# An output product in which 6 of 16 row pairs are done as seven block products instead of eight

## The chip, the cores and the metric

The kernel runs on one core of one Trainium2 chip. The metric is the device time of one execution in microseconds (us). TensorE (PE) multiplies, VectorE (DVE) and ScalarE (ACT) work elementwise, SyncE (SP) starts most transfers. Each engine works through its own list of instructions in order. The list is the order in which the program's text records them, so an instruction that waits holds back everything behind it on its engine.

## The reference, cut to what matters

One layer of a bidirectional encoder for 256 positions of width 4096. A normalised input is multiplied by `w_in` (4096 x 14336), the columns go to a convolution branch and an attention branch, and the two results, 2048 columns each and each multiplied by a gate, are multiplied together with `w_out`:

```python
h = einsum('bsd,de->bse', rms_norm(x, norm_g), w_in)
c_val, c_glu, c_gate, q, k, v, a_gate = split(h, split_pts, axis=-1)
conv_out = conformer_conv(c_val, c_glu, ...) * silu(c_gate)
attn_out = longnet_mixture(norm(q), norm(k), v, rel_bias) * silu(a_gate)
mixed = concatenate([conv_out, attn_out], axis=-1)      # 256 x 4096
x = x + einsum('bse,ed->bsd', mixed, w_out)             # the output product
```

Everything is float32.

## The kernel before, in words

**Products.** The contraction of 4096 is cut into 32 steps of 128 (`KT`), the columns into 18 groups of 1024 (`GROUPS`: 4 conv, 4 pairs of agv and qk, 2 gate, 4 out). A step of a group reads a 128x1024 piece of the weights (`raw`, loaded in pairs of steps, 1 MB each, three buffers) and makes 12 matmuls of 128x512: two halves of the columns (`e`), two halves of the positions (`s`), and three products each. The three come from a split of each float32 operand into a rounded high part and a low remainder: high by high, low by high, high by low. The stationary side is the 128x128 slice of the activations (`xh`, `xl` in the input groups, `mh`, `ml` in the out groups), the moving side the weights (`wh`, `wl`).

**The split of the weights.** `split_w` (L189) does it three steps ahead: ACT rounds 128x1024 into `wh` (L197), DVE subtracts to get `wl` (L198). There are four buffers of each, so a cast for a later step waits until PE has used up the buffer of an earlier one.

**Side work.** Between the steps `pump()` (L539) records a portion of the elementwise work: lanes of generators, each with a budget of DVE and ACT time per step (`DVE_STEP`, `ACT_STEP` = 950, 1400 ns). The order of the lanes is `mix_lane` (the split of the mixed columns), `fg` (three generators wide: attention heads and gates), `conv_lane`. Gates, queries and keys are turned into the other layout by `turn` (L289): two DVE transposes and 16 ACT copies.

**The out groups.** The mixed columns become `mh`, `ml` (`mix_split_gen`, L522), 32 tiles of 128x256, in the order 0 to 31, each as soon as the last input group has given its buffer free. The four out groups accumulate in PSUM over all 32 steps, in `acc` banks. At a group's end `add_out` (L552) adds the bank to the input tile `xr` on DVE and sends it out.

Of the kernel before, what the change touches and what calls it, by code (L numbers as in the profile page):

```python
# [32 lines left out]
DVE_STEP, ACT_STEP = 950, 1400  # L33
# [13 lines left out]
GROUPS += [("out", og, 1024 * og, 1024 * og + 512) for og in range(4)]  # L47

# [56 lines left out]
def layer_kernel(  # L105
# [8 lines left out]
    out,  # L114
# [58 lines left out]
    def load_pair(j, cuts=(0, 2048), between=None):  # L173
# [4 lines left out]
        if groups[g][0] == "out":  # L178
            jj = (jj + n_pairs // 2) % n_pairs
# [8 lines left out]

    def split_w(n):  # L189
        if n >= NG * KT:  # L190
            return
        j, kk = divmod(n, 2)
        src = raw_tiles[j][:, kk]
        wh = sb.tile([P, 1024], F32R, tag="wh", bufs=AHEAD + 1, name=f"wh{n}")
        wl = sb.tile([P, 1024], F32R, tag="wl", bufs=AHEAD + 1, name=f"wl{n}")
# [96 lines left out]
    def turn(tile_, name, flip=False):  # L292
# [226 lines left out]

    def mix_split_gen():  # L520
        for kk in range(KT):
            while not (kk in mix_ready and progress["in"] >= kk + 2):  # L522
                yield
            h, l = new_split(kk, "m")
            src = mix_ready[kk]
            nc.scalar.copy(h, src)
            nc.vector.tensor_sub(l, src, h.bitcast(F32))
            mh[kk], ml[kk] = h, l
            yield 335

    fg, mix_lane, conv_lane = Lane(3), Lane(1), Lane(1)
# [19 lines left out]
    def add_out(g, e, s, acc, queues=(nc.sync,)):  # L551

        c, n = groups[g][2 + e], 512 // len(queues)
        for i, queue in enumerate(queues):
            t = xr_tiles[(g, e)][:, s, n * i : n * i + n]
            nc.vector.tensor_add(t, t, acc[:, n * i : n * i + n])  # L556
            queue.dma_start(out[0][P * s : P * s + P, c + n * i : c + n * i + n], t)

    def evacuate(g, e, accs):
        kind, idx = groups[g][:2]  # L560
        rstd = state.get("rstd")
        if kind == "out":
            for s in range(2):
                add_out(g, e, s, accs[s])
            return
# [20 lines left out]
        elif kind == "gate":  # L586
            fg.add(gate_post(2 * idx + e, tile_))
# [14 lines left out]
    def last_products(n):  # L602

        g, k = divmod(n, KT)
        wh, wl = (t[:, 512:] for t in w_split[n])
        for s in range(2):
            a = accs[(g, 1)][s]
            hs, ls = (t[:, P * s : P * s + P] for t in (mh[k], ml[k]))
            nc.tensor.matmul(a, hs, wh, start=False, stop=False)
            nc.tensor.matmul(a, ls, wh, start=False, stop=False)  # L610
            nc.tensor.matmul(a, hs, wl, start=False, stop=True)
            add_out(g, 1, s, a, (nc.scalar, nc.sync) if s else (nc.sync,))

    def products(n, e, part):
# [6 lines left out]
        if g < n_in:  # L621
            h, l = xh[k], xl[k]
        else:
            while k not in mh:
                pump()
            h, l = mh[k], ml[k]
# [9 lines left out]
        if part == 1:  # L636
            if k == KT - 1:
                evacuate(g, e, accs.pop((g, e)))
            if e == 1:
                del w_split[n]  # L640

# [16 lines left out]
    for n in range(NG * KT):  # L658
        g, k = divmod(n, KT)
        if g == n_in - 1:  # L660
            progress["in"] = k
        elif g >= n_in:
            progress["in"] = KT + 2
        if groups[g][0] == "out" and k in (8, 12):
            e = (k - 8) // 4
            c = groups[g][2 + e]
            t = t4(f"xr{g}_{e}").rearrange("p a b -> p (a b)").rearrange("p (s c) -> p s c", s=2)
            nc.sync.dma_start(t, xs[:, :, c : c + 512])
            xr_tiles[(g, e)] = t
# [8 lines left out]
        else:  # L678
# [8 lines left out]
            split_w(n + AHEAD)  # L687
            if k < KT - 1:
                products(n, 0, 1)
            elif n < NG * KT - 1:  # L690
                products(n, 1, 0)
                products(n, 1, 1)
            else:
                last_products(n)
# [13 lines left out]


# [58 lines left out]
```

## Time and profile before

| what | us |
|---|---|
| median of three runs | 1610.34 (1609.34 to 1611.03) |
| the profiled execution, its own time | 1610.65 |
| its span, first to last instruction | 1608.9 |
| PE busy | 1602.5 |
| DVE busy | 1072.5 |
| ACT busy | 926.4 |
| out groups on PE | from 1256.4 to 1604.6 |

The profile was taken in one execution. The time outside the span (1610.65 less 1608.9) is start and end of the program. A busy PE in this profile only says that matmuls follow each other; their pace is read from their starts.

### The profile page before, as it was taken

The numbers are of one execution on the slowest core, as the hardware profiler recorded it, in microseconds if no ns is written. First come the engines' busy times: TensorE is split into PE (matmuls) and PEld (weight loads), VectorE is DVE, ScalarE is ACT, GpSimd is POOL, SyncE is SP. The second block draws the span as 40 slices with busy tenths as digits, with TensorE's granted clock in tenths as the row PEclk, the third lists the DMA queues.
The fourth block names the chain that finished last, engine by engine and source line by source line (L and its number), as shares of the span: only waits on it lengthen the run. The fifth ranks groups of instructions, "written<-read, shape, count | busy, mean of one in ns | idle before, by whom it ended". The sixth has DMA issues, their size and how long they took to land.

```text
span 1608.9 us, 18840 instructions
## 1 busy us (share of the span) xinstructions
PE 1602.5 (100%) x7058; PEld 1326.6 (82%) x7058; DVE 1072.5 (67%) x1442; ACT 926.4 (58%) x1413; POOL 0.2 (0%) x4
## 2 busy tenths in 40 slices
PE   9999999999999999999999999999999999999999
PEld 7888888888888888888888888888888888888887
DVE  6658888888888888678756555555465665454543
ACT  6763544545453456774778756774767963333332
POOL 0000000000000000000000000000000000000000
PEclk9999999999999999999999999999999999999999
DMA  9755555555555555545555555455555556566662
GB/s 372 291 185 201 191 189 203 185 185 206 187 205 184 196 197 193 193 168 199 185 195 187 187 198 197 174 189 202 184 198 188 196 204 231 207 228 216 216 229 105
DMA packets 52892, 323.53 MB, mean 201 GB/s; under 512 B 5792, under 2 KB 8480, under 8 KB 16192
## 3 DMA queue, kind: packets, MB, share of 16 engines
q1 hardware_dynamic: 52512, 322.05, 56.0%
q8 instruction: 55, 0.90, 0.2%
q10 hardware_dynamic: 288, 0.28, 0.1%
q14 instruction: 37, 0.30, 0.1%
HBM read 318.08 MB, written 4.23 MB: 200 GB/s over the span
## 4 chain that ended last, share of the span: by engine, by line
PE 98%; ACT 1%; DMA 0%; issue 0%; DVE 0%; DVEq 0%
PE acc L632 32%; PE acc L633 32%; PE acc L635 32%; PE psc L469 1%; PE po L508 1%; ACT cT L394 0%; ACT wh L197 0%; DMA first_x<-in_x_cols_dram 0%; ACT qk L308 0%; DVE wl L198 0%; DVE xr L556 0%; DVE qk L449 0%; ACT xh L245 0%; PE vapm L366 0%; PE mupm L366 0%
## 5 line engine op out<-in xcount | busy, mean ns | idle before, releaser
L198 DVE TENSOR_TENSOR wl<-raw,wh 128x1024 fp32r<-128x1024 f32 x575 | 703.6, 1224 | 514.3 <-ACT wh L197 510.4
L197 ACT CAST wh<-raw 128x1024 fp32r<-128x1024 f32 x575 | 604.9, 1053 | 638.4 <-PE acc L633 449.4
L632 PE MATMUL acc<-wh,xh 128*128 128x512 f32 x1792 | 703.9, 393 | 1.0 <-ACT xh L245 1.0
L633 PE MATMUL acc<-wh,xl 128*128 128x512 f32 x1792 | 698.6, 390 | 0.0
L635 PE MATMUL acc<-wl,xh 128*128 128x512 f32 x1792 | 484.1, 389 | 0.0
L632 PEld LDWEIGHTS acc<-wh,xh 128*128 128x128 f32 x1792 | 336.9, 188 | 71.0 <-ACT xh L245 1.3
L633 PEld LDWEIGHTS acc<-wh,xl 128*128 128x128 f32 x1792 | 337.0, 188 | 70.4 <-DVE xl L246 0.2
L635 PEld LDWEIGHTS acc<-wl,xh 128*128 128x128 f32 x1792 | 336.8, 188 | 70.5
L340 DVE SCALAR_TENSOR_TENSOR cT<-conv,wT,cT 128x241 f32<-128x241 f32 (+14 forms) x480 | 201.6, 471 | 0.0
L632 PE MATMUL acc<-wh,mh 128*128 128x512 f32 x510 | 198.4, 389 | 0.0
L633 PE MATMUL acc<-wh,ml 128*128 128x512 f32 x510 | 198.4, 389 | 0.0
L635 PE MATMUL acc<-wl,mh 128*128 128x512 f32 x510 | 137.5, 389 | 0.0
L633 PEld LDWEIGHTS acc<-wh,ml 128*128 128x128 f32 x510 | 95.8, 188 | 19.9
L635 PEld LDWEIGHTS acc<-wl,mh 128*128 128x128 f32 x510 | 95.7, 188 | 19.8
L632 PEld LDWEIGHTS acc<-wh,mh 128*128 128x128 f32 x510 | 95.7, 188 | 19.8
L499 ACT COPY pr<-turn_p 32x128 f32<-32x128 f32 x256 | 75.9, 296 | 5.9 <-DVE turn_p L493 2.4
L308 ACT COPY qk<-turn_q 32x256 f32<-32x256 f32 x64 | 25.9, 404 | 1.2
L308 ACT COPY qk<-turn_k 32x256 f32<-32x256 f32 x64 | 25.8, 403 | 1.2 <-DVE turn_k L300 0.2
L308 ACT COPY gate<-turn_g 32x256 f32<-32x256 f32 x64 | 25.9, 404 | 1.0
L308 ACT COPY agv<-turn_ag 32x256 f32<-32x256 f32 x64 | 25.8, 404 | 1.0
L308 ACT COPY conv<-turn_a 32x256 f32<-32x256 f32 x64 | 25.8, 403 | 1.1
L483 ACT ACTIVATE pr<-pr,nm 128x256 f32<-128x256 f32 x32 | 16.0, 502 | 2.5 <-DVE nm L480 2.4
(128 smaller groups left out, 402.2 us busy)
## 6 DMA issues: line engine op xcount, KB each, us to landing
raw<-in_w_dram SPq DMA_DIRECT2D x286, 1024.0 KB, 4.8
x<-in_x_dram SPq DMA_DIRECT2D x8, 512.0 KB, 7.4
xr<-in_x_dram SPq DMA_DIRECT2D x8, 512.0 KB, 5.8
out_dram<-xr SPq DMA_DIRECT2D x15, 256.0 KB, 5.2
xT<-in_x_cols_dram SPq DMA_DIRECT2D x7, 512.0 KB, 7.3
T<-bias_dram SPq DMA_DIRECT2D x16, 192.0 KB, 5.0
raw<-in_w_dram SPq DMA_DIRECT2D x3, 512.0 KB, 6.5
raw<-in_w_dram SPq DMA_DIRECT2D x2, 256.0 KB, 4.2
```

The source lines that it names most:

```text
L197: nc.scalar.copy(wh, src)
L198: nc.vector.tensor_sub(wl, src, wh.bitcast(F32))
L308: nc.scalar.copy(dst[32 * b : 32 * b + 32, :, :, to, :], backwards(v) if flip else v)
L340: nc.vector.scalar_tensor_tensor(c[:, t, lo:hi], a[:, t, lo + sh : hi + sh], wT[:, ch, k : k + 1], c[:, t, lo:hi], op0=ALU.mult, op1=ALU.add,)
L469: nc.tensor.matmul(psc[:, it, :], qt[hg][:, hh, P * it : P * it + P], kt[hg][:, hh, :], start=True, stop=True,)
L483: nc.scalar.activation(pi[:, it, :], pi[:, it, :], AF.Exp, bias=nm[:, it : it + 1], accum_out=z[:, it : it + 1],)
L499: nc.scalar.copy(dst[32 * b : 32 * b + 32, :, :, 3 - a, :], backwards(blocks[32 * a : 32 * a + 32, :, :, b, :]),)
L508: nc.tensor.matmul(po[:, :S], vt[hg][:, jt, hs], pT[:, jt, :], start=jt == 0, stop=jt == 1)
L632: nc.tensor.matmul(a, hs, wp, start=k == 0, stop=False)
L633: nc.tensor.matmul(a, ls, wp, start=False, stop=False)
L635: nc.tensor.matmul(a, hs, wp, start=False, stop=k == KT - 1)
```

## The change

The output product is written anew as a class `Out`. The rows of `w_out` are taken as 16 pairs of steps, and a pair, a column group and both position halves are a 2x2 by 2x2 block product: positions (2 halves) by steps (2), steps (2) by column halves (2). In ten pairs it stays eight block products (24 matmuls). In the six pairs 0 to 5 (heads 0 to 11) it becomes seven (21 matmuls), on sums and differences of the blocks. The weights' sums are made in each group on DVE (`t13`, `t24`), the activations' sums once (`mix_fuse`). Four of the seven results have banks of their own, m1, m5, m6 and m7, and `add_more` adds them to the right outputs after the last of the six pairs. The buffers of `wh` and `wl` become one ring of eight (`ws`), and two more buffers are taken from another pool from the eleventh pair of the first group on. The side work changes too: gates have a lane of their own ahead of `fg`, the split of mixed columns takes whatever pair is ready, in the order of use, up to twice per `pump`, and stands behind `fg`; during the two gate groups the budgets are 1300 and 1600; `turn` reports its copies in units of four instead of two.

The core of the diff:

```diff
-DVE_STEP, ACT_STEP = 950, 1400
+STEP, GATE_STEP = (950, 1400), (1300, 1600)
...
+FUSED = (0, 1, 2, 3, 4, 5)
+OUT_ORDERS = [(8, 9, 10, 0, 6, 1, 11, 2, 7, 3, 12, 4, 13, 5, 14, 15)]
+OUT_ORDERS += 3 * [(8, 9, 0, 10, 1, 11, 2, 6, 3, 7, 4, 12, 5, 13, 14, 15)]
+W_SLOTS, W_MORE = 8, 2
...
-                if a % 2 == 1:
-                    yield 0, 620
+            yield 0, 1240
...
+    def mix_fuse(j):
+        a0, a1 = mix_ready[2 * j], mix_ready[2 * j + 1]
+        a11, a21, a12, a22 = a0[:, :P], a0[:, P:], a1[:, :P], a1[:, P:]
...
+        nc.vector.tensor_add(s1, a21, a22)
+        nc.vector.tensor_sub(s2, s1, a11)
+        yield 400
+        nc.vector.tensor_sub(s3, a11, a21)
+        nc.vector.tensor_sub(s4, a12, s2)
+        yield 400
...
+        for (h, l), src in zip(parts, (a11, s1, a1, sums[:, P:])):
             nc.scalar.copy(h, src)
             nc.vector.tensor_sub(l, src, h.bitcast(F32))
+            yield 300, 300
...
     def pump():
-        for i, quota in enumerate((DVE_STEP, ACT_STEP)):
+        for i, quota in enumerate(GATE_STEP if progress["in"] >= 0 else STEP):
             left[i] = min(left[i] + quota, quota)
-        mix_lane.step(left)
+        gate_lane.step(left)
         fg.step(left)
+        for _ in range(2):
+            mix_lane.step(left)
...
+    class Out:
...
+        def step(self, most=W_SLOTS):
+            if not self.todo or sum(self.held.values()) + self.todo[0][0] > most:
+                return False
...
+        def split_plain(self, u):
+            def part(k):
...
+                nc.scalar.copy(h, src)
+                nc.vector.tensor_sub(l, src, h.bitcast(F32))
...
+        def split_fused(self, u):
...
+            def one():
...
+                nc.vector.tensor_sub(t13, r[:, 1:4:2, :], r[:, 0:2, :])
+                h, l = both("b", r[:, 0:3:2, :])
+                low(h, l, r[:, 0:3:2, :])
...
+            def two():
...
+                h, l = both("t13", t13)
+                nc.vector.tensor_sub(t24[:, 0, :], r[:, 3, :], t13[:, 0, :])
+                low(h, l, t13)
...
+            def three():
+                nc.vector.tensor_sub(t24[:, 1, :], r[:, 2, :], t24[:, 0, :])
...
+                nc.scalar.copy(hl[:, 0, :], r[:, 3, :])
+                low(hl[:, 0, :], hl[:, 1, :], r[:, 3, :])
...
+            def four():
+                h, l = both("t24", kept["t24"])
+                low(h, l, kept["t24"])
...
+        def triple(self, acc, a, b, start, stop):
+            nc.tensor.matmul(acc, a[0], b[0], start=start, stop=False)
+            nc.tensor.matmul(acc, a[1], b[0], start=False, stop=False)
+            nc.tensor.matmul(acc, a[0], b[1], start=False, stop=stop)
+        def before(self):
+            while self.step(W_SLOTS + (W_MORE if self.settled else 0)):
+                pass
...
+            rows = (
+                (more["m1"], "a11", "b11", ""), (one["c11"], "a12", "b21", "b"),
+                (more["m5"], "s1", "t1", ""), (more["m7"], "s3", "t3", "t13"),
+                (one["c12"], "s4", "b22", "b22"),
+                (more["m6"], "s2", "t2", ""), (one["c21"], "a22", "t4", "t24"),
+            )
...
+        def add_more(self, g, more):
...
+            nc.scalar.copy(m1, more["m1"])
+            nc.vector.tensor_add(r[0][1], r[0][1], more["m5"])
+            nc.vector.tensor_add(r[1][1], r[1][1], more["m5"])
+            nc.vector.tensor_add(u, m1, more["m6"])
+            nc.vector.tensor_add(v, u, more["m7"])
+            for dst, src in ((r[0][0], m1), (r[0][1], u), (r[1][0], v), (r[1][1], v)):
+                nc.vector.tensor_add(dst, dst, src)
```

**PE in an out group.** Before, 12 matmuls in a row in the third out group, as many as a step has; a pair has two such lists (`acc` the four banks, `wh` and `wl` the split weights, `mh` and `ml` the split mixed columns):

```order
L632 MATMUL acc_0_0_10991<-wh_11241,mh_9838 128x512
L633 MATMUL acc_0_0_10991<-wh_11241,ml_9839 128x512
L632 MATMUL acc_0_1_10992<-wh_11241,mh_9838 128x512
L633 MATMUL acc_0_1_10992<-wh_11241,ml_9839 128x512
L632 MATMUL acc_1_0_11009<-wh_11225,mh_9812 128x512
L633 MATMUL acc_1_0_11009<-wh_11225,ml_9813 128x512
L632 MATMUL acc_1_1_11010<-wh_11225,mh_9812 128x512
L633 MATMUL acc_1_1_11010<-wh_11225,ml_9813 128x512
L635 MATMUL acc_1_0_11009<-wl_11226,mh_9812 128x512
L635 MATMUL acc_1_1_11010<-wl_11226,mh_9812 128x512
L635 MATMUL acc_0_0_10991<-wl_11242,mh_9838 128x512
L635 MATMUL acc_0_1_10992<-wl_11242,mh_9838 128x512
```

Of the change, in the first out group, the last four of the seven block products of pair 0 (`m` a bank of its own, `c` a bank of the output, `mx` the split sums of the mixed columns):

```order
L782 MATMUL m_0_9979<-t13h_9921,mx_9228 128x512
L783 MATMUL m_0_9979<-t13h_9921,mx_9228 128x512
L784 MATMUL m_0_9979<-t13l_9922,mx_9228 128x512
L782 MATMUL c_0_9817<-b22s_9948,mx_9228 128x512
L783 MATMUL c_0_9817<-b22s_9948,mx_9228 128x512
L784 MATMUL c_0_9817<-b22s_9948,mx_9228 128x512
L782 MATMUL m_0_9978<-t24h_9980,mx_9228 128x512
L783 MATMUL m_0_9978<-t24h_9980,mx_9228 128x512
L784 MATMUL m_0_9978<-t24l_9981,mx_9228 128x512
L782 MATMUL c_0_9816<-t24h_9980,mh_9226 128x512
L783 MATMUL c_0_9816<-t24h_9980,ml_9227 128x512
L784 MATMUL c_0_9816<-t24l_9981,mh_9226 128x512
```

The matmuls keep their shape and come in threes into one bank; such a pair has 21 of them, and the whole list of PE has 72 fewer.

**DVE in the second out group.** Before, the list holds only the low parts, two for each pair:

```order
L198 TENSOR_TENSOR wl_11294<-raw_11211,wh_11293 128x1024
L198 TENSOR_TENSOR wl_11310<-raw_11211,wh_11309 128x1024
L198 TENSOR_TENSOR wl_11328<-raw_11245,wh_11327 128x1024
L198 TENSOR_TENSOR wl_11344<-raw_11245,wh_11343 128x1024
L198 TENSOR_TENSOR wl_11362<-raw_11279,wh_11361 128x1024
```

Of the change, one fused pair and the plain pair behind it (`t_20` are the sums t13 and t24, `b22s` holds the high and the low part of one block, `oh` and `ol` the split of a plain pair):

```order
L748 TENSOR_TENSOR t_20_10667<-raw_10569 128x1024
L736 TENSOR_TENSOR bl_10670<-raw_10569,bh_10669 128x1024
L759 TENSOR_TENSOR t_20_10676<-raw_10569,t_20_10667 128x512
L736 TENSOR_TENSOR t13l_10678<-t_20_10667,t13h_10677 128x1024
L765 TENSOR_TENSOR t_20_10676<-raw_10569,t_20_10676 128x512
L736 TENSOR_TENSOR b22s_10689<-raw_10569,b22s_10689 128x512
L736 TENSOR_TENSOR t24l_10705<-t_20_10676,t24h_10704 128x1024
L717 TENSOR_TENSOR ol_0_10723<-raw_10627,oh_0_10722 128x1024
L717 TENSOR_TENSOR ol_1_10733<-raw_10627,oh_1_10732 128x1024
```

Seven instructions now stand where two stood; the low part of t24 comes last and needs ACT's high part of the sum that DVE made two places ahead.

**ACT at the first fused pair of the first out group.** Of the change (`turn_g` is the turned gate, `mix_sums` and `agv` feed the split of the mixed columns, `t_3` the sums of the weights):

```order
L732 CAST bh_9898<-raw_9770 128x1024
L315 COPY gate_0_9789<-turn_g_9837 32x2x4x32 x4
L570 CAST mx_9867<-mix_sums_9841 128x384
L732 CAST t13h_9921<-t_3_9896 128x1024
L315 COPY gate_0_9789<-turn_g_9837 32x2x4x32 x4
L767 CAST b22s_9948<-raw_9770 128x512
L315 COPY gate_0_9789<-turn_g_9837 32x2x4x32 x4
L570 CAST mh_9967<-agv_0_6233 128x128
L570 CAST mh_9967<-mix_sums_9942 128x128
L732 CAST t24h_9980<-t_3_9920 128x1024
```

The casts that PE needs now share ACT's list with the copies of the third gate and the casts of the mixed columns' sums.

More of the change, by code (lines that the diff above doesn't have):

```diff
@@ L113, in layer_kernel @@
     bias_rows,
-    out,
+    y,
 ):
@@ L657, in layer_kernel @@
     split_w(1)
-    for n in range(NG * KT):
+    for n in range(n_in * KT):
         g, k = divmod(n, KT)
[L660 to L669, printed above, removed]
+        if groups[g][0] == "gate":
+            progress["in"] = max(k - KT * (n_in - 1 - g), 0)
         if n == 0:
@@ L707, in layer_kernel @@
         pump()
+    progress["in"] = KT + 2
+    out.run()
 def _layout(i):
```

222 lines of the change are left out of this document (184 added, 38 removed).

## The prediction

> **What bounds the kernel now.** First the busy times and the chain of work that ended last, from the page:
>
> ```profile
> PE 1602.5 (100%) x7058; PEld 1326.6 (82%) x7058; DVE 1072.5 (67%) x1442; ACT 926.4 (58%) x1413; POOL 0.2 (0%) x4
> PE 98%; ACT 1%; DMA 0%; issue 0%; DVE 0%; DVEq 0%
> ```
>
> A busy PE proves little in this profile, since pipelined matmuls count as busy. So next the waits, asked for PE alone. These are all there are:
>
> ```profile
> PE spin L653 <- DVE ones L136: 1.0, 1, 1.0
> PE acc L632 <- ACT xh L245: 1.0, 1, 1.0
> PE psc L469 <- DVE qk L449: 0.4, 1, 0.4
> ```
>
> In the out groups PE waits for nothing. Its pace there comes from the first and the last start, with the counts (510 + 510 + 510 + 6 = 1536 matmuls):
>
> ```profile
> L632 PE MATMUL acc<-wh,mh x510: 389/389/389, 1256.6 to 1602.5; 128*128 128x512 f32 x170
> L611 PE MATMUL acc<-wl,mh x2: 388/388/389, 1603.9 to 1604.6; 128*128 128x512 f32 x2
> ```
>
> 348.0 us over 1535 intervals is **226.7 ns for each matmul**. The 389 ns is one matmul's latency, not its pace. PE is the bound, and a matmul less is 226.7 ns less, as long as its operands are there.
>
> Whether they stay there is a question for DVE and ACT, stage by stage: the last gate group, then the four out groups (columns: PE, PEld, DVE, ACT, POOL busy us):
>
> ```profile
> 1165.00:1256.40 91.40, 91.40 (x404) 75.64 (x404) 56.52 (x77) 69.63 (x148) 0.00 (x0) 1.00 0.51 182
> 1256.40:1343.50 87.10, 87.10 (x386) 72.12 (x385) 54.84 (x74) 63.01 (x108) 0.00 (x0) 1.00 0.59 207
> 1343.50:1430.60 87.10, 87.10 (x386) 72.13 (x385) 41.58 (x37) 33.82 (x33) 0.00 (x0) 1.00 0.62 218
> 1430.60:1517.70 87.10, 87.10 (x386) 72.13 (x385) 41.58 (x37) 33.81 (x33) 0.00 (x0) 1.00 0.62 217
> 1517.70:1604.80 87.10, 87.10 (x385) 71.90 (x384) 39.16 (x35) 30.39 (x29) 0.00 (x0) 1.00 0.52 185
> ```
>
> DVE is half idle in three out groups and carries leftover side work in the first. This room is what the change spends.
>
> **What is removed.** Six pairs in four groups lose three matmuls each: 6 x 4 x 3 = 72, and 72 x 226.7 ns = **16.3 us**. A group then has 366 matmuls, 83.0 us. The new ones have the old shape. They come in threes into one bank; the nearest rows are the last six of before, which do that:
>
> ```profile
> 1604.11 0.39 PE L609 MATMUL acc<-wh,mh 128*128 128x512 f32 x1
> 1604.34 0.39 PE L610 MATMUL acc<-wh,ml 128*128 128x512 f32 x1
> 1604.57 0.39 PE L611 MATMUL acc<-wl,mh 128*128 128x512 f32 x1
> ```
>
> They start 0.23 us apart, to the two digits shown. I take the same pace, and keep for the upper end 0.0013 us for each of the 1464 matmuls, 1.9 us.
>
> **What is added on DVE.** Prices by width:
>
> ```profile
> L198 DVE TENSOR_TENSOR wl<-raw,wh 128x1024 fp32r<-128x1024 f32 x575 | 703.6, 1224 | 514.3 <-ACT wh L197 510.4 <-PE acc L635 1.9 <-PE acc L633 1.5
> L205 DVE TENSOR_TENSOR wl<-raw,wh 128x512 fp32r<-128x512 f32 x2 | 1.3, 683 | 0.0
> L527 DVE TENSOR_TENSOR ml<-agv,mh 128x256 fp32r<-128x256 f32 x16 | 6.7, 418 | 0.0
> L300 DVE STREAM_TRANSPOSE turn_g<-gate 128x512 f32<-128x512 f32 x8 | 5.6, 699 | 0.0
> L197 ACT CAST wh<-raw 128x1024 fp32r<-128x1024 f32 x575 | 604.9, 1053 | 638.4 <-PE acc L633 449.4 <-DVE cT L340 149.8 <-issue 13.0
> L203 ACT CAST wh<-raw 128x512 fp32r<-128x512 f32 x1 | 0.6, 627 | 0.3 <-DMA raw<-in_w_dram 0.3
> ```
>
> A plain pair costs DVE 2 x 1.224 = 2.45 us. A fused pair costs 4 x 1.224 + 3 x 0.683 = 6.95 us; ACT pays 3 x 1.053 + 0.627 = 3.79. Fused and plain pairs alternate in the middle of a group: 9.39 us of DVE beside 45 matmuls, 10.20 us of PE. On top comes a wait inside the fused pair: ACT's cast of t24 can start only when DVE has made the second half of t24, and DVE has one 0.683 us instruction to do meanwhile: 1.053 - 0.683 and two hand-overs of 0.04 (the cast that starts at 1450.40 below ends at 1451.45, the subtraction starts at 1451.49) make 0.45 us.
>
> ```profile
> 1450.40 1.05 ACT L197 CAST wh<-raw 128x1024 fp32r<-128x1024 f32 x1 [1.67 <-PE acc L633]
> 1451.49 1.23 DVE L198 TENSOR_TENSOR wl<-raw,wh 128x1024 fp32r<-128x1024 f32 x1 [1.50 <-ACT wh L197]
> ```
>
> So 9.84 of 10.20 us are taken: **groups two to four fit, with 0.36 us left per two pairs**. By group it is 41.58 + 6 x 4.50 + 8 x 0.683 (add_more) = 74.0 us against 83.0. A gain or loss elsewhere on ACT costs nothing there: 33.8 + 6 x 1.68 + 0.63 = 44.5 us.
>
> **The first out group does not fit.** Counted in DVE's list between its first matmul and its last: 44 instructions of 1024 columns, 26 of 512, 4 transposes, 19 of 256, 13 of 128 and 3 of 384. The last two widths are not in the trace; by the step from 256 to 512 (0.265 us) they are 0.29 and 0.55. The sum is 53.9 + 17.8 + 2.8 + 7.9 + 3.8 + 1.7 = **87.9 us**; with six waits of 0.45, 90.6, against 83.0 of PE: 7.6 us too much. The excess is no early debt that is paid back within the group; the second group opens with four `add_out` (2.7 us) and fused pairs from its third on, so DVE stays late.
>
> What covers it is how far ahead DVE may work, the ring of eight. With the tiles in order of use (four of a plain pair, seven of a fused), the low part of t24 goes where the high part of the plain pair's second step was, whose last use is matmul 44 of the 45; it is first needed by matmul 63. That is 18 matmuls, 4.1 us, and the next plain pair's first low part has 18 too. With ten tiles the tightest has 24, 5.4 us. DVE may be late by that much before PE stops.
>
> ACT adds to the lateness. Before, in the first 44 us of the out groups, it was already full, and PE did not wait:
>
> ```profile
> 1254.00:1265.00 11.00, 11.00 (x50) 9.09 (x49) 6.81 (x8) 10.73 (x21) 0.00 (x0) 1.00 0.45 157
> 1265.00:1276.00 11.00, 11.00 (x50) 9.11 (x49) 8.24 (x14) 9.86 (x18) 0.00 (x0) 1.00 0.59 220
> 1276.00:1287.00 11.00, 11.00 (x50) 9.10 (x49) 7.08 (x9) 10.66 (x21) 0.00 (x0) 1.00 0.67 244
> 1287.00:1298.00 11.00, 11.00 (x50) 9.12 (x49) 7.34 (x13) 10.71 (x22) 0.00 (x0) 1.00 0.67 239
> ```
>
> Now the copies of the third gate stand between the casts of the first fused pair, and DVE, which could once run past, needs those casts in order. I take between 0 and 2 us of DVE time lost there, and 1.0 as the value.
>
> Stalls of PE in the first group and at the start of the second: 7.6 + 1.0 - 4.1 = **4.5 us**, in many pieces of less than 2 us. Bounds: 0 (the work ahead and the ten tiles cover all) and 10 (nothing covered).
>
> **The last gate group.** By the lists it gets about 10 us more on each engine (DVE 56.5 to 67, ACT 69.6 to 79 of 91.4). These are the casts and sums of pairs 0 to 2 and a gate that is turned earlier. A late cast there has 28 matmuls, 6.3 us, from the last use of its buffer to its own use; the running excess of ACT over PE, added step by step from the list, peaks at 4.4. I take no cost, with 0 to 2 us.
>
> **Edits at nothing.** The loads of weights keep their number, and 1 MB lands in 4.8 us where a buffer of three has more than 9. `add_more` (5.5 us of DVE) stands where three to five plain pairs follow, which leave DVE 3 us each. The mixed columns are recorded at least two pairs ahead of use. If one of these covers were gone, PE would wait for that one instruction, 1 to 2 us. The tail, last matmul to the end, has the same two halves and queues.
>
> ```profile
> raw<-in_w_dram SPq DMA_DIRECT2D x286, 1024.0 KB, 4.8
> ```
>
> **Sum.** 1610.65 (1608.9 of span and 1.75 around it) - 16.3 + 4.5 = **1598.8 us**. The profiled execution is 0.3 above the median of the three runs; that is within the runs' own spread, and I leave it.
>
> **The rivals.**
>
> *All is covered.* DVE starts the out groups with nothing outstanding and the larger budgets have emptied the lanes. Against it: 7.6 us of excess is more than either cover. Time: 1610.65 - 16.3 = 1594.3.
>
> *A jam of ACT and DVE.* Casts late in the gate group and in the first out group add up and nothing is made good: 10 us instead of 4.5: 1604.
>
> *One long stall.* If the lateness falls on one wait, PE restarts slowly. The trace has one such restart, after the wait at the start:
>
> ```profile
> 5.41 0.80 PE L632 MATMUL acc<-wh,xh 128*128 128x512 f32 x1 [1.02 <-ACT xh L245]
> 6.00 0.73 PE L633 MATMUL acc<-wh,xl 128*128 128x512 f32 x1
> 6.53 0.63 PE L632 MATMUL acc<-wh,xh 128*128 128x512 f32 x1
> 6.96 0.63 PE L633 MATMUL acc<-wh,xl 128*128 128x512 f32 x1
> 7.38 0.63 PE L632 MATMUL acc<-wh,xh 128*128 128x512 f32 x1
> 7.81 0.63 PE L633 MATMUL acc<-wh,xl 128*128 128x512 f32 x1
> 8.23 0.63 PE L632 MATMUL acc<-wh,xh 128*128 128x512 f32 x1
> 8.66 0.63 PE L633 MATMUL acc<-wh,xl 128*128 128x512 f32 x1
> 9.09 1.47 PE L635 MATMUL acc<-wl,xh 128*128 128x512 f32 x4
> 10.39 0.39 PE L632 MATMUL acc<-wh,xh 128*128 128x512 f32 x1
> ```
>
> They start 0.43 us apart before they fall to 0.227. The twelve ahead of 10.39 took 4.98 us instead of 2.72: 2.3 us, so 1601.1. The windows show a granted clock of 1.00 in every stage here, so nothing but the start bears on it, and my stalls are short. The Trainium skill, in "TensorE: Matmul & The Clock Gate" (section "Why this matters for your kernels"), says that a gap of PE over about 3 us sends the clock back to half; that speaks against any change that trades matmuls for waits. By that rule single stalls below its limit cost only themselves, which leaves the sum at 1598.8. The slow start at 5.41 agrees with it in size; a gap in mid-kernel is not shown here.
>
> *DVE becomes the bound in all four groups (slower).* The place is the wait for t24's cast. The 0.45 us holds only if ACT is free at that moment and the other casts stay hidden. A fused pair may lose 0.81 us (10.20 - 9.39) before each further bit is paid 24 times. At 1.49 us (0.81 + 16.3/24) the whole gain is gone. If the cast of t13 is exposed too (1.053 + 0.08), the loss is 1.58 us or a little over; at 1.7 it is 24 x 0.89 = 21.4 us more than 1594.3: 1615.7. For it: DVE waited for such casts 501 times before, 510.4 us. Against it: that was an idle engine early at its post, and behind t13's cast DVE has 1.224 us of other work.
>
> That the matmuls are not removed can be excluded: PE's list has 72 rows fewer.
>
> **How the numbers follow.** Forecast 0.58, all covered 0.13, jam 0.10, long stall 0.06, DVE bound everywhere 0.13. The predicted time is the forecast's. The range takes in full cover (1594.3) and the upper bounds together (10 of stalls, 1.9 of pace, less a little): 1594 to 1607, and leaves out the DVE bound and little else. A measurement of this kernel tells about 0.2%, 3.2 us, from no change: faster is below 1607.1. All of the forecast but 0.01, full cover, nearly all of the jam and the long stall, and a little of the last rival make 0.86; the rest is 0.06 for the same and 0.08 for slower, both mostly the last rival.
>
> **What would show it.** The profile after should have PE's pace at 0.227 in the out groups, DVE near 88 us in the first of them and 74 in the second and third, waits of PE for DVE's low parts (t24's, and the plain pair's behind it) of 2 to 8 us in all, from the fourth pair of the first group to about the fourth of the second, and none in the gate groups. Waits spread over all groups would mean the last rival; waits for ACT in the gate group the jam; starts 0.43 us apart the long stall. Wrong altogether would be a pace that is not 0.227, or a fused pair that costs DVE more than 7.4 us.

## The result, and the profile after

The changed kernel takes **1603.47 us** (median, 1603.11 to 1603.91), the kernel before on the same chip 1610.31 (1609.34 to 1611.03). The ratio is **0.9959, 95% interval 0.9944 to 0.9973**: faster by 0.4%, 6.8 us, of the 16.3 us that the removed matmuls are worth. The profiled execution took 1603.12 us, with a span of 1601.3. One disturbed execution, of e5 below (2692.08 us at a granted clock of 0.557, one of five), is left out of its median.

First the busy times and the chain, from the page of the changed kernel:

```profile
PE 1590.5 (99%) x6986; PEld 1312.8 (82%) x6986; DVE 1195.0 (75%) x1630; ACT 968.2 (60%) x1480; POOL 0.2 (0%) x4
PE 96%; ACT 1%; DVE 1%; issue 0%; DMA 0%; DVEq 0%; ACTq 0%
```

PE has 72 matmuls fewer (7058 - 6986). The first and last start in the out groups, from the instructions by line:

```profile
L782 PE MATMUL c<-oh,mh x320: 387/389/628, 1257.8 to 1596.5; 128*128 128x512 f32 x160
L784 PE MATMUL c<-ol,mh x320: 388/389/628, 1258.2 to 1597.0; 128*128 128x512 f32 x160
```

The out groups last from 1257.8 to 1597.0. 1463 intervals of 0.2267 us would be 331.7 of these 339.2 us, so **7.5 us are lost in the out groups**. They also start 1.1 us later than before (1257.8 against 1256.6 us, first matmul against first matmul; the 1256.4 in the table of before is the weight load ahead of it). -16.3 + 7.5 + 1.1 is -7.7 us; the spans differ by -7.6.

Which stages lose it? The last gate group and the four out groups (columns: PE, PEld, DVE, ACT, POOL busy us, granted clock, DMA share, GB/s):

```profile
1165.00:1257.80 92.80, 92.03 (x404) 75.21 (x403) 63.91 (x109) 79.91 (x175) 0.00 (x0) 1.00 0.51 180
1257.80:1348.30 90.50, 86.91 (x367) 69.16 (x366) 80.89 (x110) 62.35 (x99) 0.00 (x0) 0.98 0.53 194
1348.30:1431.30 83.00, 83.00 (x368) 68.70 (x367) 72.19 (x78) 42.78 (x46) 0.00 (x0) 1.00 0.69 245
1431.30:1514.30 83.00, 83.00 (x368) 68.73 (x367) 70.15 (x74) 43.08 (x46) 0.00 (x0) 1.00 0.64 228
1514.30:1597.30 83.00, 83.00 (x367) 68.46 (x365) 66.74 (x71) 39.10 (x42) 0.00 (x0) 1.00 0.50 179
```

The windows are cut at each group's first matmul. Groups two to four take 83.0 us each, and PE never pauses in them. The first takes 90.5: all 7.5 us are there. Its DVE is busy for 80.9 us, less than PE would need without a pause (83.0); ACT is idle for 28 us. Over the whole group no engine is full, and yet PE waits. But DVE is nearly full: its 9.6 idle us are all waits for ACT (10.2 us by the list of waits, the largest of them below), so its work and these waits fill the group between them. PE's waits behind 1150 us:

```profile
PE m L782 <- ACT t24h L732: 1.2, 1, 1.2
PE m L784 <- DVE t24l L736: 1.1, 3, 0.5
PE po L514 <- ACT pr L505: 0.8, 2, 0.5
PE c L782 <- ACT oh L716: 0.5, 1, 0.5
PE c L784 <- DVE ol L717: 0.5, 1, 0.5
PE m L784 <- DVE t13l L736: 0.2, 1, 0.2
```

The waits for `pr` (turned attention weights) are in the gate group, the others in the first out group. The listed waits of the first out group, 3.5 us, are shorter than the loss. A wait is counted from the modelled end of the matmul before, which is later than the next start at full pace; the start behind it follows after 0.33 to 0.34 us instead of 0.227; and behind two of the waits several starts stand 0.43 us apart (last section). What held DVE and ACT back there, over 1257 to 1345 us:

```profile
DVE t24l L736 <- ACT t24h L732: 4.1, 5, 2.0
DVE ol L717 <- ACT oh L716: 3.5, 4, 1.3
```

```profile
ACT mh L547 <- DVE cT L416: 10.3, 5, 3.4
ACT t24h L732 <- DVE t L765: 4.9, 3, 2.0
```

**DVE waits for ACT, and ACT waits for DVE.** ACT's list around the largest of these waits shows how:

```profile
1284.29 0.41 ACT L547 CAST mh<-cT 128x256 fp32r<-128x256 f32 x1 [3.43 <-DVE cT L416]
1284.60 1.05 ACT L732 CAST t13h<-t 128x1024 fp32r<-128x1024 f32 x1
1285.55 0.61 ACT L767 CAST b22s<-raw 128x512 fp32r<-128x512 f32 x1
1287.27 0.41 ACT L547 CAST mh<-cT 128x256 fp32r<-128x256 f32 x1 [1.11 <-DVE cT L416]
1288.81 0.41 ACT L547 CAST mh<-cT 128x256 fp32r<-128x256 f32 x1 [1.13 <-DVE cT L416]
1289.12 1.04 ACT L732 CAST t24h<-t 128x1024 fp32r<-128x1024 f32 x1
```

The cast of a mixed column stands in ACT's list behind the DVE multiplication by the gate that makes it (L416), which DVE has recorded behind the weights' subtractions. ACT waits 3.43, 1.11 and 1.13 us for it, and the casts that PE needs next (`t13h`, `t24h`) stand behind it. PE stops for `t24h` until 1290.22 and for `t24l` until 1291.48 (its rows are in the last section).

A second place has another cause. The copies of a turn stand between the casts of one fused pair, and DVE meets them at `t24h`:

```profile
1307.35 1.65 ACT L315 COPY gate<-turn_g 32x256 f32<-32x256 f32 x4
1309.03 0.62 ACT L767 CAST b22s<-raw 128x512 fp32r<-128x512 f32 x1
1309.67 1.65 ACT L315 COPY gate<-turn_g 32x256 f32<-32x256 f32 x4
1311.34 1.05 ACT L732 CAST t24h<-t 128x1024 fp32r<-128x1024 f32 x1
```

```profile
1309.68 0.69 DVE L736 TENSOR_TENSOR b22s<-raw,b22s 128x512 fp32r<-128x512 f32 x1 [0.19 <-ACT b22s L767]
1312.42 1.22 DVE L736 TENSOR_TENSOR t24l<-t,t24h 128x1024 fp32r<-128x1024 f32 x1 [2.05 <-ACT t24h L732]
```

PE itself hardly stops here (one start 0.34 us behind the one before). Its next stops come from 1324 to 1328 us, and ahead of those ACT has again waited for `cT`: 3.33 us until 1318.89 and 1.33 us until 1324.90. So the second group of stops has both causes behind it.

### The profile page after: what moved, and what is told of

It is laid out like the page before. It is cut to its first block, busy times and chain, and to the rows that moved or that the text cites. A ratio compares the mean times of both kernels' runs of the same rounds, so it can differ in the third digit from the quotient of the medians.

```text
span 1601.3 us, 18984 instructions
## 1 busy us (share of the span) xinstructions
PE 1590.5 (99%) x6986; PEld 1312.8 (82%) x6986; DVE 1195.0 (75%) x1630; ACT 968.2 (60%) x1480; POOL 0.2 (0%) x4
## 4 chain that ended last, share of the span: by engine, by line
PE 96%; ACT 1%; DVE 1%; issue 0%; DMA 0%; DVEq 0%; ACTq 0%
PE acc L662 25%; PE acc L663 25%; PE acc L665 25%; PE c L784 5%; PE c L782 5%; PE c L783 5%; PE m L784 1%; PE m L782 1%; PE m L783 1%; PE po L514 1%; PE psc L475 1%; ACT gate L315 0%; ACT pr L505 0%; DMA first_x<-in_x_cols_dram 0%; DVE t24l L736 0%
## 5 line engine op out<-in xcount | busy, mean ns | idle before, releaser
L205 DVE TENSOR_TENSOR wl<-raw,wh 128x1024 fp32r<-128x1024 f32 x447 | 546.9, 1224 | 336.9 <-ACT wh L204 335.9
L204 ACT CAST wh<-raw 128x1024 fp32r<-128x1024 f32 x447 | 469.6, 1052 | 434.9 <-PE acc L663 241.5
L782 PE MATMUL c<-oh,mh 128*128 128x512 f32 x320 | 125.3, 391 | 0.5 <-ACT oh L716 0.5
L784 PE MATMUL c<-ol,mh 128*128 128x512 f32 x320 | 125.1, 391 | 0.5 <-DVE ol L717 0.5
L783 PE MATMUL c<-oh,ml 128*128 128x512 f32 x320 | 125.0, 391 | 0.0
L716 ACT CAST oh<-raw 128x1024 fp32r<-128x1024 f32 x80 | 83.2, 1051 | 50.8 <-PE c L783 34.4
L717 DVE TENSOR_TENSOR ol<-raw,oh 128x1024 fp32r<-128x1024 f32 x80 | 96.1, 1222 | 21.8 <-ACT oh L716 15.2
L782 PEld LDWEIGHTS c<-oh,mh 128*128 128x128 f32 x320 | 60.5, 189 | 13.5 <-ACT oh L716 1.0
L784 PEld LDWEIGHTS c<-ol,mh 128*128 128x128 f32 x320 | 60.3, 189 | 13.5 <-DVE ol L717 1.0
L783 PEld LDWEIGHTS c<-oh,ml 128*128 128x128 f32 x320 | 60.5, 189 | 12.8
L732 ACT CAST bh<-raw 128x1024 fp32r<-128x1024 f32 x24 | 25.3, 1053 | 16.3 <-PE m L783 16.3
```

The costliest lines, as they stand in the source:

```text
L204: nc.scalar.copy(wh, src)
L205: nc.vector.tensor_sub(wl, src, wh.bitcast(F32))
L782: nc.tensor.matmul(acc, a[0], b[0], start=start, stop=False)
L783: nc.tensor.matmul(acc, a[1], b[0], start=False, stop=False)
L784: nc.tensor.matmul(acc, a[0], b[1], start=False, stop=stop)
```

## The experiments

The theory tested: the loss comes from the order in which fused casts and side work stand in the lists of ACT and DVE (**order**). Its rivals: DVE has too much to do in the first group (**throughput**), or the ring of buffers is too short (**cover**). Where expectations speak of A and A1, that is the order; A2 is throughput. All times are medians, and the ratio is to the kernel before on the same chip. Differences of about 1 us are near the limit: the thousandth matmul, up to which all these kernels have the same matmuls, starts between 229.7 and 231.6 us in their profiled executions.

| kernel | us | ratio to before, 95% interval |
|---|---|---|
| the changed kernel | 1603.47 | 0.9959 (0.9944 to 0.9973) |
| e1: no pair fused | 1612.43 | 1.0013 (1.0004 to 1.0023) |
| e2: mixed columns cast later | 1599.77 | 0.9936 (0.9921 to 0.9951) |
| e3: ten tiles from the start | 1602.97 | 0.9955 (0.9938 to 0.9972) |
| e4: two gates not turned | 1596.51 | 0.9913 (0.9898 to 0.9928) |
| e5: turns in units of two | 1604.09 | 0.9962 (0.9948 to 0.9976) |
| e6: t24 whole at once | 1602.43 | 0.9951 (0.9936 to 0.9966) |
| e7: e2 and e6 | 1598.67 | 0.9929 (0.9913 to 0.9946) |
| e8: small gate budgets | 1602.57 | 0.9953 (0.9938 to 0.9968) |
| e9: e7 and e8 | 1602.65 | 0.9951 (0.9936 to 0.9966) |
| e10: e7, fused pairs one pair later | 1597.56 | 0.9920 (0.9905 to 0.9935) |
| e11: e9 and e10 | 1601.41 | 0.9945 (0.9928 to 0.9961) |
| e12: first group not fused | 1598.47 | 0.9928 (0.9910 to 0.9946) |

**e1, the new program without any fused pair.**

```diff
-FUSED = (0, 1, 2, 3, 4, 5)
+FUSED = ()
```

> Everything of the change but the seven-product pairs: all 16 pairs are done as eight products, with the new lanes, budgets, ring and order of pairs. The loss of 8.6 us against 72 matmuls saved is 1.1 us ahead of the out groups and 7.4 in the first one. Theory A (the fused pairs' work on DVE and ACT meets the side work in the first group): without fused pairs nothing waits in the out groups and only the 1.1 us of the gate group stay: 1611 to 1612, ratio 1.0005 to 1.001. Rival (the new lanes and the new order make the waits by themselves): the first out group still loses several us, 1614 to 1618.

1612.43 us: 2.0 more than before on the same chip (1610.39), with the same matmuls, and 0.4 above the range of the theory. PE waits nowhere in its out groups; what it waits for late in the program is in the gate group:

```profile
PE po L514 <- ACT pr L505: 1.6, 2, 1.0
```

So the new order of the side work costs about 2 us ahead of the out groups (the last 410 matmuls there take 95.4 us, before 92.9) and nothing in them. The stalls of the first out group come with the fused pairs.

**e2, the cast of a gate's mixed column three pumps after the multiplication at the earliest.**

```diff
+LAG = 3
...
             mix_ready[NH + 4 * cb + t] = cT[cb][:, t, :]
+            ready_at[NH + 4 * cb + t] = pumps[0]
...
                 if 2 * j in mix_ready and 2 * j + 1 in mix_ready:
-                    break
+                    if pumps[0] >= ready_at.get(2 * j + 1, 0) + LAG:
+                        break
...
     def pump():
+        pumps[0] += 1
```

> Same work, one order changed: the casts of the mixed columns of the last two gates are recorded three portions later than the multiplication that makes them, so that ACT does not reach them before DVE has done it. Theory A1 (ACT, in order, waits 1.1 to 3.4 us for a late DVE multiplication, and the casts of t13 and t24 behind it come late, which makes DVE wait in turn): the two clumps of waits, around 1290 and 1325 us, shrink by half or more; 1599 to 1601. Rival A2 (DVE simply has more work than PE leaves time for): the order does not matter, 1603 within 0.7.

1599.77 us, 3.7 less than the changed kernel, for the same work. The four executions scatter from 1598.91 to 1602.22; all lie below the fastest of the changed kernel (1603.11). The profiled one is the slowest of them, and the clock fell in it (last section). ACT's waits for `cT` (10.3 us before this edit) are gone from the list of waits; its longest is now

```profile
ACT t13h L736 <- DVE t L752: 8.8, 4, 2.3
```

That a reordering alone gives back 3.7 us speaks for order, and against throughput as the only cause.

**e3, two more tiles in the ring from the first out group's start** (`self.settled = True` instead of `False`).

> The two further tiles for split weights may be used from the start of the out groups instead of from the eleventh pair. The cover grows from 18 to 24 matmuls, by 1.3 us. A2 (lateness grows steadily until it exceeds the cover): one time 1.3 us less, 1602. A1 (two separate clumps, each made by one blocked cast): the first clump alone has the new cover, 1.3 to 2 us less, and no clock drop behind it; 1600.5 to 1602. If the cover were not the matter at all: 1603.5.

1602.97 us, in none of the ranges; the interval overlaps that of the changed kernel nearly whole, and in the profiled execution the out groups lose 8.1 us, not less than 7.5. How far DVE may work ahead matters little: what holds it is not a full ring.

**e4, gates three and four not turned.**

```diff
-        yield from turn(g, f"turn_g{cb}")
+        if cb < 2:
+            yield from turn(g, f"turn_g{cb}")
```

> Leaves out the turn of the third and fourth gate (4 transposes, 2.8 us of DVE; 32 copies, 12.9 us of ACT), all of which lie in the first out group; the gates are multiplied unturned. A2 (amount of work): stalls fall by the 2.8 us of DVE and more for the copies that stood between the casts: 1599 to 1600. A1 (the blocked casts): multiplications and casts of the mixed columns are still there and only come earlier; the clumps stay at more than half: 1601.5 to 1603.

1596.51 us, 7.0 less, lower than any theory had it. One wait is left to PE in the out groups:

```profile
PE m L785 <- DVE t24l L737: 0.5, 1, 0.5
```

These turns are 2.8 us of work on DVE (4 x 0.70) and 13.2 on ACT (32 copies, 1.65 for four) in a group in which ACT had 28 us idle. This run does not tell order from throughput. Over the first group DVE has a little less to do (79.2 us instead of 81.0), and its waits for ACT are 5.6 us instead of 10.2; and throughput (1599 to 1600) forecast the larger gain, nearer to the measured one than order (1601.5 to 1603). Two gates less also move everything behind them, so both places of the first section are taken away at once.

**e5, turns in units of two copies.**

```diff
-            yield 0, 1240
+                if a % 2 == 1:
+                    yield 0, 620
```

> The turns go back to units of two copies; everything else is the changed kernel. Theory A (order coupling: waits arise where ACT's side work stands between the fused casts or ACT waits behind a late DVE instruction): fewer copies stand between two casts, so DVE's waits for t24's cast get shorter (the largest was 2.05 us), while the wait of ACT for the late gate multiplication stays: 1602.0 to 1603.5. Rival B (the units of four bring the gates forward, and that is needed): the gates get later and the first out group carries more: 1604.5 to 1607.

1604.09 us, no gain. The rival was right in kind: with smaller units more side work is left for the first out group (DVE has 85.4 us to do there instead of 81.0), and PE waits for the mixed columns themselves:

```profile
1331.96 0.49 PE L783 MATMUL c<-oh,mh 128*128 128x512 f32 x1 [1.72 <-ACT mh L548]
1334.46 0.79 PE L784 MATMUL c<-oh,ml 128*128 128x512 f32 x1 [2.01 <-DVE ml L549]
```

So the units of four, which lengthen DVE's wait for `t24h`, are also what keeps the last mixed columns ahead of their use. The time itself stays a little under what the rival gave (from 1604.5 on).

**e6, both halves of t24 made together, ahead of t13's low part.**

```diff
                 nc.vector.tensor_sub(t24[:, 0, :], r[:, 3, :], t13[:, 0, :])
+                nc.vector.tensor_sub(t24[:, 1, :], r[:, 2, :], t24[:, 0, :])
                 low(h, l, t13)
...
-                nc.vector.tensor_sub(t24[:, 1, :], r[:, 2, :], t24[:, 0, :])
```

> The second half of t24 is made directly behind the first, so that 1.9 us of DVE work instead of 0.68 stands between it and the low part that needs its cast. If the wait inside the fused pair (priced at 0.45 us, six times in the first group) is what makes PE stall, it goes: 1600.8 to 1602. Theory A: it is the side work in ACT's list, and only the smaller part of the waits goes: 1602 to 1603. Rival A2 (DVE's total work): the sum of work is the same, 1603.5.

1602.43 us: 1.0 less than the changed kernel, within what order gave. The interval overlaps with that of the changed kernel, so this edit alone is not settled.

**e7, e2 and e6 together.**

> Both the lag of three pumps between a gate's multiplication and the cast of its column (1599.77 alone) and the earlier second half of t24. Theory A: the remaining waits, all for t24, lose most of their length: 1597.8 to 1599. Rival A2 (what is left is DVE's total work): as the lag alone, 1599.5 to 1600.

1598.67 us, 1.1 below e2 alone, at the upper end of what order gave. The size of e6's effect is seen twice, each time near what the measurement can tell. In the profiled execution the out groups lose 3.7 us instead of 7.5; over the first group DVE has almost the same to do (80.2 us, before the two edits 81.0) and waits less (7.3 us instead of 10.2). This is the cleanest evidence for order.

**e8, the gate groups' budgets back at 950 and 1400.**

```diff
-STEP, GATE_STEP = (950, 1400), (1300, 1600)
+STEP, GATE_STEP = (950, 1400), (950, 1400)
```

> The budgets in the gate groups go back to 950 and 1400 ns a pump; everything else is the changed kernel. If the 1.1 to 1.5 us lost in the gate group come from the larger budgets (ACT overfilled there), they go, but more side work is left for the first out group: theory A expects the balance slower, 1604.5 to 1608. Rival: the first out group is bound to its own fused work and a little more side work is covered: 1602 to 1603.

1602.57 us, 0.9 less where order expected more. The intervals overlap, so a gain is not shown; the loss that order expected is not there, and the rival's range holds. The windows of e8 over the gate group and the first out group:

```profile
1165.00:1257.00 92.00, 92.00 (x408) 76.28 (x407) 59.37 (x90) 77.74 (x166) 0.00 (x0) 1.00 0.53 187
1257.00:1345.00 88.00, 82.36 (x349) 64.29 (x348) 81.70 (x126) 63.06 (x107) 0.00 (x0) 1.00 0.53 191
```

The waits in the gate group are gone (PE 92.00 of 92.00). In the first out group DVE has 126 instructions in 88.0 us (the changed kernel 107 in the same window), and PE now waits most for DVE's low parts. What is won ahead is lost behind: the last 410 matmuls ahead of the out groups take 92.9 us instead of 94.6, and the out groups lose 9.3 us instead of 7.5.

**e9, e7 with the small budgets.**

> The lag, the earlier second half of t24 (both together 1598.67), and the budgets of the gate groups back at 950 and 1400. With the larger budgets PE loses 1.5 to 2 us to late turns of attention weights in the last gate group. Theory A: this loss goes, and the side work left over meets fused casts that are now less tied to it, so about 1 us is gained: 1597 to 1598.3. Rival (the leftover adds to DVE's and ACT's excess in the first out group, which is at its limit): what is won in the gate group is lost behind it, 1598.5 to 1600.5.

1602.65 us, the same as e8 and 4.0 more than e7: the reordering that gave 4.8 us gives nothing here. The first out group of e9:

```profile
1257.00:1345.00 88.00, 82.64 (x352) 64.72 (x351) 82.12 (x129) 64.45 (x111) 0.00 (x0) 1.00 0.55 196
```

DVE is busy for 82 of 88 us, and PE gets through 352 matmuls where 388 would fit (88.0 / 0.2267). Over the whole first group, from its first matmul to the next group's, DVE is busy for 85.8 us (e8: 85.5). That is more than the 83.0 that PE needs, so with this much side work left over DVE's own load does not fit. Throughput is therefore not wrong in itself: **the changed kernel, with 81.0 us, stands just below that limit, and the large budgets keep it there**. The expected 1597 to 1598.3 was wrong for this reason; the rival (1598.5 to 1600.5) was right in kind and too low as well.

**e10, e7 with each fused pair of the first group one pair later.**

```diff
-OUT_ORDERS = [(8, 9, 10, 0, 6, 1, 11, 2, 7, 3, 12, 4, 13, 5, 14, 15)]
+OUT_ORDERS = [(8, 9, 10, 6, 0, 11, 1, 7, 2, 12, 3, 13, 4, 14, 5, 15)]
```

> The lag, the earlier second half of t24, and in the first out group another order: each fused pair stands one pair later (four plain pairs ahead of the first instead of three). Theory A (PE waits where fused casts meet the turns of the gates; more of the side work is now done while plain pairs leave DVE and ACT free): 1597 to 1598.3. Rival A2 (the excess over the whole group counts): 1598.4 to 1599. Rival: the mixed columns of the later pairs become the late ones, since the order is tuned to when they get ready: 1599.5 to 1602.

1597.56 us, the best kernel with the whole computation: 5.9 under the changed kernel and 0.9920 (0.9905 to 0.9935) of the kernel before. Where the list of waits had seven of PE in the first out group, it has two, next to the copies of a turn (the first line below lies in the gate group). By the starts the out groups lose 2.3 us:

```profile
PE po L516 <- ACT pr L507: 0.8, 2, 0.6
PE m L786 <- ACT t24h L736: 0.6, 1, 0.6
PE m L788 <- DVE t24l L740: 0.5, 1, 0.5
```

The instructions are the same, in another order, but the run does not speak for order alone. With each fused pair one pair later, `add_more` ends behind the first group: DVE has four instructions fewer in that group than in the changed kernel, and 77.7 us to do instead of e7's 80.2, while its waits do not shrink (8.6 us, in e7 7.3). The last 1.1 us, near what the measurement can tell, go with the lighter load.

**e11, e10 with the small budgets.**

> The lag, the earlier second half of t24, the small budgets and the later fused pairs together. If the effects add, 1596 to 1597.5, near the 1596.5 of the kernel without two turns. If the small budgets' leftover meets the fused pairs, or the mixed columns come late: 1598.5 to 1601.

1601.41 us, 3.9 more than e10 and a little above the second range. The budgets do the same harm as in e9: DVE has 84.4 us to do in the first group. Part of it is the clock, which fell in the profiled execution; behind 1318.7 us seven starts there are 0.43 us apart, about 1.5 us in all.

**e12, the first out group done with eight products in all pairs.**

```diff
-                make = self.split_fused if j in FUSED else self.split_plain
+                make = self.split_fused if j in FUSED and og else self.split_plain
...
-                if j in FUSED:
+                if j in FUSED and og:
...
+        for kk, (h, l) in ((2 * j, b0), (2 * j + 1, b1)):
+            mh[kk], ml[kk] = h, l
```

> Seven products only in out groups two to four; in the first the six pairs are done as eight products again, 18 matmuls more (4.1 us) than the changed kernel. The sums of the mixed columns are still made, and the first group's products use one of them in place of a quarter of the columns, so its output is not the reference's; all matmuls are there. If the later groups hide their fused work whole and everything lost is lost to the fused casts of the first group (and 1 to 2 us in the gate group): the kernel without fused pairs (1612.43) less 54 matmuls, 12.2 us, is 1600.2, so 1599.5 to 1601. Rival (the later groups or the sums themselves cost something): over 1602.

1598.47 us, 5.0 *less* than the changed kernel, with 18 matmuls more. The output is not the reference's, since one of the sums stands in for a quarter of the columns; the matmuls are all there. The time came out 1 us under the expectation, which was reckoned from e1; e1's longest wait in the gate group is 1.0 us, here it is 0.5. In the out groups PE waits for nothing:

```profile
1257.00:1345.00 88.00, 88.00 (x390) 72.88 (x389) 55.94 (x77) 54.47 (x87) 0.00 (x0) 1.00 0.61 220
```

So the six fused pairs of the first group save 4.1 us of matmuls and cost 9.1 (5.0 + 4.1) by the medians. By the spans of the profiled executions it is 8.6 (1601.3 - 1596.8 + 4.1), of which 7.5 are lost in the first out group. Most of the rest is not theirs: 0.7 is there at the thousandth matmul (it starts at 230.8 and 230.2 us), and 0.3 lies behind the last matmul's start. Fused in groups two to four alone, the seven products cost nothing. In the order of e10 the first group seems worth fusing too: e10 is 0.9 us below e12, with overlapping intervals, and its out groups lose 2.3 us for the 4.1 of matmuls that are saved.

**Order and load together.** Over the first group, DVE's busy time and all its waits add up to the group's length to within 1.0 us in each of these runs: 81.0 + 10.2 in the changed kernel (90.6 us long), 80.2 + 7.3 in e7 (86.7), 77.7 + 8.6 in e10 (85.3), 79.2 + 5.6 in e4 (83.8), 85.8 + 6.2 in e9 (91.7). Nearly all of these waits are for ACT (in e9, 2.0 us are for PE). The sum says how the time is filled, not which wait cost how much. But it shows two ways to shorten the group, less work on DVE and shorter waits, and neither order nor throughput is the whole cause: 81.0 us of work leave 2.0 of the 83.0 for waits, and in the order of the changed kernel there are 10.2.

## Why the prediction was right and wrong

The measured 1603.5 us lies in the range, 4.7 above the forecast of 1598.8. The sign and the place were right; a term of the sum was mis-sized, and its working was wrong. That the stalls came out within 3 us is luck: an excess of work that is not there (7.6 us) stood in for waits that were not counted.

- **Removed, 72 x 226.7 ns = 16.3 us: right.** 72 rows are gone, and groups two to four take 83.0 us each, as forecast. The pace in triples is the old one.
- **Groups two to four fit, with 74.0 us of DVE: right.** 72.2 and 70.2 in the second and third, no wait of PE. This excludes the rival in which DVE becomes the bound everywhere.
- **The first out group does not fit, 87.9 us of DVE against 83.0: the number was wrong.** I multiplied counts by durations. But DVE's instructions overlap when they follow each other. Four in a row of the changed kernel:

```profile
1335.58 4.63 DVE L717 TENSOR_TENSOR ol<-raw,oh 128x1024 fp32r<-128x1024 f32 x4
1340.12 0.68 DVE L880 TENSOR_TENSOR xr<-xr,m 128x512 f32<-128x512 f32 x1
1340.72 0.68 DVE L881 TENSOR_TENSOR xr<-xr,m 128x512 f32<-128x512 f32 x1
1341.32 0.68 DVE L882 TENSOR_TENSOR us<-m1s,m 128x512 f32<-128x512 f32 x1
1342.03 0.69 DVE L883 TENSOR_TENSOR vs<-us,m 128x512 f32<-128x512 f32 x1
```

  One lasts 1.22 us, but four are through in 4.63 (a start every 1.137), and two of 512 columns start 0.60 apart, not 0.68. My list at these paces (0.63, 0.34, 0.21 and 0.47 for transposes, 256, 128 and 384 columns, by the same reading) is 44 x 1.137 + 26 x 0.60 + 2.5 + 6.5 + 2.7 + 1.4 = 78.7 us. Measured: 80.9 in the window above. DVE's work alone fits into 83.0, with 2 us to spare. The Trainium skill, "VectorE: DVE Perf Modes", section "The DRAIN you can't avoid", says that the next operation does not start until the pipe is empty, and that one that is not held starts earlier. The rows agree with the second for instructions that do not read each other's result: they start 0.09 us before the one ahead has ended. Where one does (`vs` reads `us`, 0.71 us after it), it starts behind the end.
- **Cover of 4.1 us by the ring: a term that did not decide.** Two tiles more in e3 changed the time by 0.5 us.
- **ACT adds 0 to 2 us of lateness, taken as 1.0: this step failed.** I saw that copies stand between casts and took it for small. In the first out group DVE waits about 10 us for ACT (4.1, 3.5, and 2.6 in smaller groups), and ACT waits 10.3 us for `cT`, which I had not seen at all: a mixed column, recorded as soon as its multiplication was recorded, puts a wait on late DVE work ahead of the casts that DVE needs. e2 takes this away and gains 3.7, e7 4.8. The stalls are 7.5 us instead of 4.5, and the way I got 4.5 (an excess of work less a cover) is not how they arise.
- **The wait of 0.45 us inside the fused pair: small, as priced.** e6 gives it more than enough cover and gains 1.0 us, with overlapping intervals.
- **The last gate group at 0, bounds 0 to 2: at the wrong end of its bounds.** The out groups start 1.1 us later (1.6 by the last 410 matmuls ahead of them); e8 removes PE's waits there.
- **Mixed columns recorded at least two pairs ahead: true as changed.** The later of pair 14's two casts starts at 1318.9 us, its first matmul at 1337.5. In e5 this cover is used up: the cast starts at 1334.1, and PE waits 2.0 us.
- **The rivals.** The jam of ACT and DVE (1604) named the right pair of engines and the right stages, and came nearer than the forecast; I gave it 0.10. Its sign, waits for ACT in the gate group, is there too (0.8 us). Full cover is refuted, the slow restart is in the last section.
- **The signs**: in the first out group PE stops seven times by the list, each time for under 2 us and from the fourth pair on, as said. None lies beyond that group, where some were expected. The waits for DVE's low parts are 1.8 us (2 to 8 expected), and 1.7 more are for ACT's high parts, which the forecast did not name.

Not settled: of the 8.7 us that e9's out groups lose, 2.8 are DVE's load by itself (85.8 us against 83.0); how the waits make up the rest was not taken apart. The waits for `cT` were taken away alone, by e2; the copies of a turn between the casts were not.

## What to carry to other kernels

Price an elementwise engine by the distance of its starts in a run of such instructions, not by durations, and then ask not only whether the work of a stage fits, but what stands between two instructions that another engine waits for in turn. Where two engines work in lists of fixed order and hand work to each other both ways, put a step of side work into the consumer's list only when its producer is surely done: three pumps of delay gave back 3.7 us here. The two questions are one sum: the fuller the engine is, the less of its waits can hide. And use a saving that needs free engines only in the stages in which they are free: in e12 it wins 5.0 us more without the first group than the changed kernel with it.

## What the hardware showed that I had not expected

The granted clock fell in the middle of the changed kernel after two short waits. Window and PE's list in the first out group:

```profile
1290.00:1300.00 10.00, 9.25 (x32) 7.17 (x33) 9.80 (x11) 5.69 (x8) 0.00 (x0) 0.83 0.52 202
```

```profile
1288.50 0.50 PE L784 MATMUL c<-b22s,mx 128*128 128x512 f32 x1
1290.22 0.50 PE L782 MATMUL m<-t24h,mx 128*128 128x512 f32 x1 [1.22 <-ACT t24h L732]
1290.56 0.39 PE L783 MATMUL m<-t24h,mx 128*128 128x512 f32 x1
1291.48 0.50 PE L784 MATMUL m<-t24l,mx 128*128 128x512 f32 x1 [0.53 <-DVE t24l L736]
...
1292.33 0.63 PE L784 MATMUL c<-t24l,mh 128*128 128x512 f32 x1
1292.75 0.63 PE L782 MATMUL c<-oh,mh 128*128 128x512 f32 x1
...
1295.31 0.54 PE L782 MATMUL c<-oh,mh 128*128 128x512 f32 x1
1295.69 0.39 PE L783 MATMUL c<-oh,ml 128*128 128x512 f32 x1
```

No gap is longer than 1.72 us from start to start. The matmuls from 1292.33 on start 0.43 us apart; the eight intervals up to 1295.69 take 3.36 us instead of 1.81, 1.5 us more. In e5 the window from 1330 to 1340 us has a clock of 0.66, behind waits of 1.72 and 2.01 us. In e8 a gap of 1.77 us and one of 0.92 behind it left the clock at 1.00, so the length of the waits alone does not say when it falls. In e2 it fell behind gaps of 1.42 and 0.92 us. The Trainium skill, "TensorE: Matmul & The Clock Gate", section "Why this matters for your kernels", puts the limit at a gap of about 3 us; here it fell with no gap above 1.72 us, so short waits close together count too. The clock is not what the loss hangs on: the profiled execution of e3 lost as much (8.1 us in the out groups) with a clock of 1.00 throughout, and the two executions of the changed kernel with a mean clock of 1.000 took 1603.83 and 1603.91 us, no less than the others.
